# Two-layer decoder trunk: norm steps pinned to fixed places among the products, and an output projection whose second half starts with the weights still held

## The chip, the cores and the metric

The kernel runs on one core of a Trainium2 chip. The metric is the device time of one execution in microseconds (us), lower is better; the time before is the median of three runs. The core's engines are named as the profile names them: PE (TensorE, the matrix products), DVE (VectorE), ACT (ScalarE), POOL (GpSimd) and SP (SyncE, which here only issues transfers, in its own order). Each engine works through its own list of instructions in order.

## The reference, cut to what matters

```python
for l in range(2):                              # x: (1, 1024, 1024) float32
    hn = rms_norm(h, norm_mix_pre[l])
    ...                                         # l == 0: RG-LRU recurrence, l == 1: sliding-window attention -> y (768 wide)
    m_out = memory_attention(mq, mk, mv)        # 256 wide
    mixed = jnp.concatenate([y, m_out], axis=-1) @ w_out[l]
    h = h + rms_norm(mixed, norm_mix_post[l])
    f = swiglu_ffn(rms_norm(h, norm_ffn_pre[l]), w_ffn_in[l], w_ffn_out[l])
    h = h + rms_norm(f, norm_ffn_post[l])
```

Between the output projection (`w_out`) and the feed-forward stand two norms in a row: one of `mixed`, and, after the residual is added, one of `h`. Both need a sum of squares over all 1024 channels before the first feed-forward product can start on a token.

## The kernel before

**Layout.** Activations are held transposed: channels on the 128 partitions (8 tiles, index k or m), tokens along the free axis in two halves of 512 (n = 0 and 1). Every float32 product is made of three products of split operands: an operand is cast to a rounded high part (ACT, names ending in h: `ah`, `wh`, `th`, `ch`) and the rest is a subtraction (DVE, names ending in l: `al`, `wl`, `tl`, `cl`). This split is line L87 (cast) and L88 (subtraction), whatever is split. One output tile of a projection is 8 x 3 = 24 products (L147 to L149).

**Output projection (`mix_out`, `mix_half`).** For half 0 of the tokens the eight output tiles m = 0 to 7 are made in order, then for half 1 again m = 0 to 7. In layer 0 the weights of half 0 are loaded raw, split, and their parts written to memory (`keep`, tensor `kept_wo`); in half 1 all eight are fetched back (`fetch`, L190). In layer 1 all sixteen are fetched (`parted_wo`). The tiles `wh`, `wl` have two buffers in layer 0 and three in layer 1, so a fetch waits until the product block two (three) before it is done. SP issues the fetches, the residual loads (L102), the spills of the new residual (`hx`, L533) and the first feed-forward weights (`wq`, `wp`, L553) in one list.

**A norm (`rstd`)** takes five steps on four engines: DVE and ACT sum the squares; PE sums over partitions with a column of ones (`rcol`, L232, output `oo`); DVE scales (L236); POOL raises to the power -1/2 (L237); PE spreads the result over the partitions (`spread`, L244, `oo<-ident,rc...`) and ACT copies it out (L248). For each half of the tokens there are two norms: `rcp` (of `mixed`) and `rcn` (of the new residual). DVE then multiplies (`post`, L530, L532) and scales (`scaled`, L540) the eight tiles, which are split again into the operands `ah`, `al` of the feed-forward.

**Feed-forward (`ffn`).** The first products (L578 to L580) take half 0; then come two blocks of a second kind (`gated`, L599 to L601), then L578 to L580 with half 1. The two norms of half 1 have to run beside the products of half 0. `place` adds order-only dependencies by which a listed product comes behind a norm step; it doesn't hold the norm step back behind earlier products.

**Last attention units of layer 1.** Sixteen attention units (a head group for half 1 of the tokens: scores `ss` L1034, transposes `tt` L1057, output products `oo` L1064) are left when `mix_out(1)` starts. They are dealt out evenly over the eight output tiles of half 0, and `attend` runs a unit's output products when a later unit has begun.

Of the kernel before, what the change touches and what calls it, by code (L numbers as in the profile page):

```python
# [7 lines left out]
F32 = mybir.dt.float32  # L8
F32R = mybir.dt.float32r
AF = mybir.ActivationFunctionType  # L10
ALU = mybir.AluOpType
# [19 lines left out]
A_PLACES, F_PLACES, END_PLACES = (36, 54), (14, 30, 104, 116), (30, 48)  # L31
# [12 lines left out]
class Trunk:  # L44
# [12 lines left out]
    def phase(self, name, psum, *pools):  # L57
# [3 lines left out]
        self.pend, self.chain, self.where = [], None, {}  # L61
# [43 lines left out]
    def attend(self, unit=None):  # L105
        depth = self.where["qs"][1] - 1
        if unit is not None:
            self.pend.append(unit())
        while len(self.pend) > (depth if unit is not None else 0):
            self.pend.pop(0)()  # L110
# [254 lines left out]
    def mem_unit(self, q, e, kv, y):  # L365
# [21 lines left out]
        def out():  # L387
# [7 lines left out]
            for m in range(2):  # L395
                ph, pl = pts[m]
                nc.tensor.matmul(o, vv[:, m, e], pl, start=m == 0, stop=False)
                nc.tensor.matmul(o, vv[:, m, e], ph, start=False, stop=m == 1)
            self.head_out(o, y, 64 * e)

# [71 lines left out]
    def mix_split(self, y, n, order):  # L472
        act = [None] * KT
# [5 lines left out]
    def mix_half(self, layer, act, n, order, ms, f, s):  # L479
        for m in ms:  # L480
            if layer or n:
                w = self.fetch(("wo", m))
            else:
                w = self.weight(self.a["wo"][layer, m])
                self.keep(("wo", m), w)
            ps = self.proj(w, [act, act], n, ks=order)
            ft = self.acc_tile()
            self.nc.scalar.copy(ft, ps)
            if m < KT - 1:
                self.sumsq(s[0], ft, m == 0)  # L490
            else:
                s.append(self.t("sq"))
                self.nc.scalar.activation(s[1], ft, AF.Square)
            f.append(ft)

    def mix_out(self, layer, y, order, src, early=(), ld=[(f"k{h}{i}",) for h in "hl" for i in range(4)]):
        f, s, act = ([], []), [None, None], [None, None]
        hx = self.dp.tile([D, T], F32, name=f"hx{layer}")
# [7 lines left out]
        a0 = self.mix_split(y, 0, order)  # L506
        s[0] = [self.t("s")]
        us = list(early)
        for m in range(KT):
            for _ in range(-(-len(us) // (KT - m))):  # L510
                self.attend(us.pop(0))
            self.mix_half(layer, a0, 0, order, [m], f[0], s[0])
        self.attend()
        a1 = self.mix_split(y, 1, order)
        s[1] = [self.t("s")]
        self.mix_half(layer, a1, 1, order, range(2), f[1], s[1])
        finish(0, self.rstd(s[0], "p")[1], ld, "s", "rsn")
        self.mix_half(layer, a1, 1, order, range(2, KT), f[1], s[1])
# [18 lines left out]
    def scaled(self, f, rs, gain):  # L537
        act = []
# [703 lines left out]
```

## Time and profile before

| | |
|---|---|
| median of three runs (lowest, highest) | 2057.79 us (2057.29, 2061.75) |
| profiled execution | 2059.32 us |
| its span in the trace | 2057.5 us |
| mean granted PE clock over the span | 0.985 |
| instructions in the span | 27844 |

The span is the traced part of the profiled execution; about 1.8 us lie around it. A granted clock of 1 is 2.4 GHz, 0.5 is 1.2 GHz; values between are means over a stretch. Layer 0's output projection and the start of its feed-forward lie at about 255 to 400 us, layer 1's last attention units, output projection and start of the feed-forward at about 1200 to 1430 us.

### The profile page before, as it was taken

The numbers are of one execution on the slowest core, as the hardware profiler recorded it, in microseconds if no ns is written. First come the engines' busy times: TensorE is split into PE (matmuls) and PEld (weight loads), VectorE is DVE, ScalarE is ACT, GpSimd is POOL, SyncE is SP. The second block draws the span as 40 slices with busy tenths as digits, with TensorE's granted clock in tenths as the row PEclk, the third lists the DMA queues.
The fourth block names the chain that finished last, engine by engine and source line by source line (L and its number), as shares of the span: only waits on it lengthen the run. The fifth ranks groups of instructions, "written<-read, shape, count | busy, mean of one in ns | idle before, by whom it ended". The sixth has DMA issues, their size and how long they took to land.

```text
span 2057.5 us, 27844 instructions
## 1 busy us (share of the span) xinstructions
PE 1976.0 (96%) x9368; PEld 1639.0 (80%) x9368; DVE 1411.4 (69%) x2313; ACT 1022.5 (50%) x1953; POOL 483.7 (24%) x476
## 2 busy tenths in 40 slices
PE   7899999999999999999999999879999999999997
PEld 6787877788888887888788878767888888888887
DVE  7877856887677676456878776669755665664566
ACT  6757774444444444454545676644333333344551
POOL 4323420114434321000035432210122322300001
PEclk9999999999999999999999999989999999999998
DMA  5422458247677789665455314162454454686653
GB/s 170 152 84 73 140 203 307 77 159 252 233 262 246 254 284 362 212 209 169 163 195 174 134 50 165 36 236 93 149 174 136 160 172 136 204 287 194 214 182 122
DMA packets 185567, 371.68 MB, mean 181 GB/s; under 512 B 20432, under 2 KB 25808, under 8 KB 185424
## 3 DMA queue, kind: packets, MB, share of 16 engines
q1 hardware_dynamic: 185424, 369.91, 53.5%
q8 instruction: 73, 1.20, 0.2%
q14 instruction: 70, 0.57, 0.1%
HBM read 259.73 MB, written 110.10 MB: 180 GB/s over the span
## 4 chain that ended last, share of the span: by engine, by line
PE 79%; DVE 8%; ACT 4%; DMA 3%; issue 3%; POOL 2%; SPq 0%; POOLq 0%; DVEq 0%; ACTq 0%
PE mm L599 12%; PE mm L601 12%; PE mm L600 12%; PE mm L707 6%; PE mm L708 6%; PE mm L709 6%; PE mm L149 5%; PE mm L147 4%; PE mm L148 4%; PE mm L578 1%; PE mm L579 1%; PE mm L580 1%; PE oo L1064 1%; DVE acc L540 1%; DVE al L88 1%
## 5 line engine op out<-in xcount | busy, mean ns | idle before, releaser
L87 ACT CAST ch<-wq 128x512 fp32r<-128x512 f32 x311 | 193.3, 621 | 437.9 <-PE mm L600 229.2
L88 DVE TENSOR_TENSOR cl<-wq,ch 128x512 fp32r<-128x512 f32 x311 | 234.2, 754 | 193.6 <-ACT ch L87 118.8
L147 PE MATMUL mm<-al,wh 128*128 128x512 f32 x616 | 249.0, 404 | 12.4 <-DVE al L936 7.6
L149 PE MATMUL mm<-ah,wl 128*128 128x512 f32 x616 | 248.0, 403 | 5.3 <-DVE wl L88 4.0
L599 PE MATMUL mm<-al,ch 128*128 128x512 f32 x640 | 252.1, 394 | 0.0
L601 PE MATMUL mm<-ah,cl 128*128 128x512 f32 x640 | 250.8, 392 | 0.0
L600 PE MATMUL mm<-ah,ch 128*128 128x512 f32 x640 | 250.1, 391 | 0.0
L148 PE MATMUL mm<-ah,wh 128*128 128x512 f32 x616 | 246.3, 400 | 0.0
L707 PE MATMUL mm<-tl,ch 128*128 128x512 f32 x532 | 207.7, 390 | 4.0 <-DVE tl L88 4.0
L708 PE MATMUL mm<-th,ch 128*128 128x512 f32 x532 | 207.1, 389 | 0.0
L709 PE MATMUL mm<-th,cl 128*128 128x512 f32 x532 | 205.2, 389 | 0.0
L599 PE MATMUL mm<-tl,ch 128*128 128x512 f32 x480 | 188.5, 393 | 0.0
L601 PE MATMUL mm<-th,cl 128*128 128x512 f32 x480 | 188.5, 393 | 0.0
L600 PE MATMUL mm<-th,ch 128*128 128x512 f32 x480 | 187.3, 390 | 0.0
L610 DVE TENSOR_TENSOR c<-c,mm 128x512 f32<-128x512 f32 x120 | 82.4, 686 | 114.3 <-PE mm L601 114.2
L147 PEld LDWEIGHTS mm<-al,wh 128*128 128x128 f32 x616 | 118.0, 192 | 39.9 <-DVE al L936 9.7
L149 PEld LDWEIGHTS mm<-ah,wl 128*128 128x128 f32 x616 | 117.7, 191 | 33.3 <-DVE wl L88 6.6
L601 PEld LDWEIGHTS mm<-ah,cl 128*128 128x128 f32 x640 | 120.1, 188 | 28.0
L600 PEld LDWEIGHTS mm<-ah,ch 128*128 128x128 f32 x640 | 120.2, 188 | 26.5
L599 PEld LDWEIGHTS mm<-al,ch 128*128 128x128 f32 x640 | 120.2, 188 | 26.0
L148 PEld LDWEIGHTS mm<-ah,wh 128*128 128x128 f32 x616 | 118.1, 192 | 23.5
L619 POOL TENSOR_TENSOR x<-wq,wq 128x512 f32<-128x512 f32 x36 | 49.1, 1364 | 338.6 <-DMA wq<-in_wi_dram 246.9
(338 smaller groups left out, 4296.2 us busy)
## 6 DMA issues: line engine op xcount, KB each, us to landing
wq<-in_wi_dram SPq DMA_DIRECT2D x168, 256.0 KB, 4.6
xz<-hd SPq DMA_DIRECT2D x154, 256.0 KB, 4.5
th<-xz SPq DMA_DIRECT2D x154, 256.0 KB, 3.6
wp<-in_wf_dram SPq DMA_DIRECT2D x112, 256.0 KB, 4.4
wz<-wp SPq DMA_DIRECT2D x88, 256.0 KB, 2.6
wq<-wz SPq DMA_DIRECT2D x56, 256.0 KB, 3.7
wraw<-in_wa_dram SPq DMA_DIRECT2D x27, 512.0 KB, 3.5
wq<-in_wf_dram SPq DMA_DIRECT2D x42, 256.0 KB, 3.7
```

Of the source, the lines that this page charges most:

```text
L87: self.nc.scalar.copy(hi, src)
L88: return (eng or self.nc.vector).tensor_tensor(lo, src, hi.bitcast(F32), op=ALU.subtract)
L147: self.mms += [nc.tensor.matmul(out, wh, al, start=i == 0, stop=False), nc.tensor.matmul(out, wh, ah, start=False, stop=False), nc.tensor. ...
L148: nc.tensor.matmul(out, wh, ah, start=False, stop=False),
L149: nc.tensor.matmul(out, wl, ah, start=False, stop=i == len(ks) - 1)]
L599: ins += [mm(out, wh, xl, start=start and k == 0, stop=False, skip_group_check=not start), mm(out, wh, xh, start=False, stop=False, skip_g ...
L600: mm(out, wh, xh, start=False, stop=False, skip_group_check=not start),
L601: mm(out, wl, xh, start=False, stop=k == 3, skip_group_check=not start)]
L610: add = lambda o, x, y: nc.vector.tensor_tensor(o, x, y, op=ALU.add)
L707: ins += [mm(ps[m], wh[:, m], xl[:, cs], start=start and p == 0, stop=False, skip_group_check=not start), mm(ps[m], wh[:, m], xh[:, cs], s ...
L708: mm(ps[m], wh[:, m], xh[:, cs], start=False, stop=False, skip_group_check=not start),
L709: mm(ps[m], wl[:, m], xh[:, cs], start=False, stop=p == NFB // 2 - 1, skip_group_check=not start)]
```

## The change

Four edits. `F_PLACES` now pins the norm steps of the feed-forward: `pin` makes a norm step wait behind its place among the products, as well as holding the products after it. The norms of half 0 are pinned in the same way among the products of half 1 (`MIX_PLACES`). Half 1 of the output projection begins with the output tiles whose weights are still in the buffers (m = 6, 7 in layer 0, 5, 6, 7 in layer 1) and fetches only the others. The last attention units go to the first six output tiles of half 0, and their output products are placed evenly among all products of that half. `scaled` orders each scaling behind the low split two tiles before, and the residual loads of layer 0 get ten buffers in place of four. Lines of the changed kernel are numbered a little higher (L88 becomes L89, L236 becomes L237, L232 becomes L233, L244 becomes L245, L530 becomes L551, L578 becomes L601, L599 becomes L622).

```diff
-A_PLACES, F_PLACES, END_PLACES = (36, 54), (14, 30, 104, 116), (30, 48)
+A_PLACES, F_PLACES, END_PLACES = (36, 54), (10, 20, 100, 110), (30, 48)
+MIX_TAIL, MIX_PLACES = 2, (10, 20, 108, 118)
...
-            self.pend.pop(0)()
+            self.outs.append(self.pend.pop(0)())
...
+    def mix_half(self, layer, act, order, steps, f, s):
+        for i, (m, w) in steps:
+            ps = self.proj(w(m), [act], 0, ks=order)
+            f[m] = self.acc_tile()
+            self.nc.scalar.copy(f[m], ps)
...
         us = list(early)
+        self.outs, self.mms = [], []
         for m in range(KT):
-            for _ in range(-(-len(us) // (KT - m))):
+            for _ in range(-(-len(us) // max(KT - MIX_TAIL - m, 1))):
                 self.attend(us.pop(0))
-            self.mix_half(layer, a0, 0, order, [m], f[0], s[0])
-        self.attend()
-        a1 = self.mix_split(y, 1, order)
+            if m == KT - MIX_TAIL:
+                self.attend()
+            done = [order[m]] if not early else order if m == KT - MIX_TAIL else []
+            self.mix_split(y, 1, done, a1)
+            self.mix_half(layer, a0, order, [(m, (m, new))], f[0], s[0])
+        for i, g in enumerate(self.outs):
+            self.place(self.mms, [[g]], [(i + 1) * len(self.mms) // (len(self.outs) + 1)])
         s[1] = [self.t("s")]
-        self.mix_half(layer, a1, 1, order, range(2), f[1], s[1])
+        steps = [(m, lambda m: held[m]) for m in range(KT - room, KT)]
+        steps += [(m, lambda m: self.fetch(("wo", m))) for m in range(KT - room)]
+        steps = list(enumerate(steps))
+        self.mms = []
+        self.mix_half(layer, a1, order, steps[:room], f[1], s[1])
+        self.marks = []
         finish(0, self.rstd(s[0], "p")[1], ld, "s", "rsn")
-        self.mix_half(layer, a1, 1, order, range(2, KT), f[1], s[1])
+        marks = self.marks
+        self.mix_half(layer, a1, order, steps[room:], f[1], s[1])
+        for i, g in zip(MIX_PLACES, marks):
+            self.pin(self.mms, i, g)
...
     def scaled(self, f, rs, gain):
-        act = []
+        act, low = [], []
         for k in range(KT):
-            self.nc.vector.scalar_tensor_tensor(f[k], f[k], self.col(gain + k), rs, op0=ALU.mult, op1=ALU.mult)
+            ins = self.nc.vector.scalar_tensor_tensor(f[k], f[k], self.col(gain + k), rs, op0=ALU.mult, op1=ALU.mult)
+            if k > 1:
+                self.after(ins, low[k - 2])
             act.append(self.act_tile())
-            self.split(*act[k], f[k])
+            low.append(self.split(*act[k], f[k]))
...
+    def pin(self, mms, i, g):
+        self.after(g[0], mms[i - 1])
+        self.place(mms, [g], [i])
...
-        self.place(mms[0] + between + mms[1], marks, F_PLACES)
+        for i, g in zip(F_PLACES, marks):
+            self.pin(mms[0] + between + mms[1], i, g)
```

**PE, start of layer 1's feed-forward.** In these rows `mm` are feed-forward products, `oo<-ones` the two partition sums of the norm `rcp` of half 1, and `oo<-ident,rcp` its spread. Before:

```order
L244 MATMUL oo_13145<-ident,rcn_2865_13141 128x128 x4
L232 MATMUL oo_13394<-ones,s_12994 128x1 x4
L232 MATMUL oo_13394<-ones,sq_13392 128x1 x4
L244 MATMUL oo_13407<-ident,rcp_13403 128x128 x4
L578 MATMUL mm_13494<-al_13153,th_2918_13446 128x512
L579 MATMUL mm_13494<-ah_13152,th_2918_13446 128x512
```

The same place after the change, from the last product ahead of the sums to the spread:

```order
L601 MATMUL mm_13471<-al_13161,th_2920_13432 128x512
L233 MATMUL oo_13368<-ones,s_12980 128x1 x4
L622 MATMUL mm_13699<-al_13161,ch_13695 128x512
L623 MATMUL mm_13699<-ah_13160,ch_13695 128x512
L624 MATMUL mm_13699<-ah_13160,cl_13696 128x512
L233 MATMUL oo_13368<-ones,sq_13366 128x1 x4
L602 MATMUL mm_13471<-ah_13160,th_2920_13432 128x512
L603 MATMUL mm_13471<-ah_13160,tl_2921_13433 128x512
L601 MATMUL mm_13468<-al_13166,th_2908_13420 128x512
```

Before, no feed-forward product stood ahead of the sums, or between the sums and the spread. Now ten products stand ahead of the first sum, three between the two sums, and ten between the second sum and the spread. The spread of `rcn` for half 0, which stood just ahead, has moved to the middle of the output projection's half 1. Layer 0 has the same order (there, before, the spread stood behind some thirty products).

**DVE, the same norm in layer 1.** `rcp` is the short step between PE's sums and POOL's power; `acc<-acc,rsp` needs the spread result. Before:

```order
L88 TENSOR_TENSOR al_13153<-acc_11945,ah_13152 128x512
L236 TENSOR_SCALAR rcp_13403<-oo_13394 128x4
L88 TENSOR_TENSOR al_13158<-acc_12109,ah_13157 128x512
L88 TENSOR_TENSOR al_13163<-acc_12281,ah_13162 128x512
L88 TENSOR_TENSOR al_13168<-acc_12453,ah_13167 128x512
L88 TENSOR_TENSOR al_13173<-acc_12556,ah_13172 128x512
L88 TENSOR_TENSOR al_13178<-acc_12659,ah_13177 128x512
L88 TENSOR_TENSOR al_13183<-acc_12762,ah_13182 128x512
L88 TENSOR_TENSOR al_13188<-acc_12865,ah_13187 128x512
L88 TENSOR_TENSOR tl_2919_13447<-wq_13462,th_2918_13446 128x512
L88 TENSOR_TENSOR tl_2921_13449<-wq_13464,th_2920_13448 128x512
L88 TENSOR_TENSOR tl_2923_13451<-wq_13470,th_2922_13450 128x512
```

After:

```order
L89 TENSOR_TENSOR al_13196<-acc_12976,ah_13195 128x512
L89 TENSOR_TENSOR cl_13696<-wq_13687,ch_13695 128x512
L89 TENSOR_TENSOR cl_13715<-wq_13689,ch_13714 128x512
L89 TENSOR_TENSOR cl_13742<-wp_13733,ch_13741 128x512
L89 TENSOR_TENSOR cl_13761<-wp_13735,ch_13760 128x512
L237 TENSOR_SCALAR rcp_13377<-oo_13368 128x4
L551 TENSOR_TENSOR acc_13228<-acc_13228,rsp_13380 128x512
L551 TENSOR_TENSOR acc_13262<-acc_13262,rsp_13380 128x512
```

Ten subtractions that could run at once stood between `rcp` and the next step of the norm; now they stand ahead of `rcp`, and what follows it waits for the spread.

**SP, the fetches of layer 0's half 1.** `wh<-kept_wo` and `wl<-kept_wo` are the two transfers of one output tile's weights. Before, around the seventh and eighth tile:

```order
L190 DMA wh_3219<-kept_wo_2783 128x1024
L190 DMA wl_3220<-kept_wo_2783 128x1024
L533 DMA hx_2511<-acc_2811 128x512
L533 DMA hx_2511<-acc_2850 128x512
L553 DMA wq_3355<-in_wi_dram 128x512
L553 DMA wq_3357<-in_wi_dram 128x512
L190 DMA wh_3253<-kept_wo_2822 128x1024
L190 DMA wl_3254<-kept_wo_2822 128x1024
```

After, ahead of the fetch for the seventh tile of the half (m = 4):

```order
L103 DMA th_712_3483<-in_xT_dram 128x512
L103 DMA th_713_3489<-in_xT_dram 128x512
L103 DMA th_714_3496<-in_xT_dram 128x512
L103 DMA th_715_3503<-in_xT_dram 128x512
L576 DMA wq_3365<-in_wi_dram 128x512
L103 DMA tl_716_3510<-in_xT_dram 128x512
L576 DMA wq_3367<-in_wi_dram 128x512
L191 DMA wh_3205<-kept_wo_2725 128x1024
L191 DMA wl_3206<-kept_wo_2725 128x1024
```

Before, two spills and two weight loads stood between the last two fetches. Now the fetch for m = 4 stands behind residual loads and behind `wq` loads that wait for a buffer of the feed-forward.

## Rows read from the trace of the kernel before

**Rows 1.** Page, part 1: busy us, share of the span, instructions.

```profile
PE 1976.0 (96%) x9368; PEld 1639.0 (80%) x9368; DVE 1411.4 (69%) x2313; ACT 1022.5 (50%) x1953; POOL 483.7 (24%) x476
```

**Rows 2.** Waits of PE, 1335 to 1430 us: total us, times, longest.

```profile
PE oo L244 <- POOL rcp L237: 11.0, 1, 11.0
PE mm L578 <- DVE al L88: 2.7, 1, 2.7
PE oo L232 <- ACT rsn L248: 0.9, 1, 0.9
```

**Rows 3.** Timeline of PE, 1366 to 1390 us: start, duration, [idle before, releaser].

```profile
1382.11 2.08 PE L244 MATMUL oo<-ident,rcp 128*128 128x128 f32 x8 [11.04 <-POOL rcp L237]
...
1385.68 0.39 PE L580 MATMUL mm<-ah,tl 128*128 128x512 f32 x1
1385.91 0.39 PE L578 MATMUL mm<-al,th 128*128 128x512 f32 x1
```

**Rows 4.** Timeline of POOL around its two slow powers.

```profile
1375.25 6.80 POOL L237 TENSOR_TENSOR rcp<-rcp,mhalf 128x4 f32<-128x4 f32 x1 [12.04 <-DVE rcp L236]
361.95 3.80 POOL L237 TENSOR_TENSOR rcp<-rcp,mhalf 128x4 f32<-128x4 f32 x1 [19.62 <-DVE rcp L236]
```

**Rows 5.** Line L237, powers of `rcp`: ns, min/median/max.

```profile
L237 POOL TENSOR_TENSOR rcp<-rcp,mhalf x7: 1008/1020/6805, 309.8 to 1987.9; 128x4 f32<-128x4 f32 x7
```

**Rows 6.** Timeline of DVE, 1368 to 1386 us.

```profile
1369.11 5.39 DVE L540 SCALAR_TENSOR_TENSOR acc<-acc,cst,rsn 128x512 f32<-128x512 f32 x8 [6.16 <-DMA wp<-in_wi_dram]
...
1375.09 4.30 DVE L88 TENSOR_TENSOR al<-acc,ah 128x512 fp32r<-128x512 f32 x7
1379.30 1.89 DVE L88 TENSOR_TENSOR tl<-wq,th 128x512 fp32r<-128x512 f32 x3
```

**Rows 7.** Timeline of PE behind its two waits on `al`.

```profile
398.24 0.50 PE L578 MATMUL mm<-al,th 128*128 128x512 f32 x1 [2.69 <-DVE al L88]
...
1422.80 0.50 PE L578 MATMUL mm<-al,th 128*128 128x512 f32 x1 [2.69 <-DVE al L88]
...
1426.48 0.46 PE L578 MATMUL mm<-al,th 128*128 128x512 f32 x1
```

**Rows 8.** Waits of PE, 285 to 405 us (layer 0).

```profile
PE oo L232 <- ACT sq L493: 2.0, 1, 2.0
...
PE oo L244 <- POOL rcp L237: 1.5, 1, 1.5
PE oo L232 <- DVE x L222: 0.9, 1, 0.9
...
PE mm L147 <- DMA wh<-kept_wo: 0.6, 1, 0.6
PE mm L149 <- DMA wl<-kept_wo: 0.5, 1, 0.5
```

**Rows 9.** Transfers issued from 296 to 352 us: count, KB, median us to landing.

```profile
wh<-kept_wo SPq DMA_DIRECT2D x8, 512.0 KB, 4.2
wl<-kept_wo SPq DMA_DIRECT2D x8, 512.0 KB, 5.4
```

**Rows 10.** Waits of PE, 1200 to 1340 us (last attention units).

```profile
PE ss L1034 <- DVE nm L1036: 2.8, 6, 0.9
PE tt L1057 <- POOL pb L1046: 2.7, 2, 2.5
PE tt L1057 <- DVE pl L88: 2.4, 2, 2.3
PE oo L232 <- DVE acc L356: 1.4, 1, 1.4
```

**Rows 11.** Windows: us; PE, PEld, DVE, ACT, POOL busy (instructions); PE clock; DMA.

```profile
1240.00:1322.00 82.00, 76.85 (x469) 66.81 (x467) 56.88 (x178) 59.39 (x166) 21.13 (x45) 0.98 0.26 91
1322.00:1340.00 18.00, 15.49 (x76) 13.09 (x77) 8.05 (x14) 8.33 (x15) 2.65 (x5) 0.81 0.27 101
```

**Rows 12.** DVE groups, 1240 to 1322 us: output of a unit.

```profile
L356 DVE TENSOR_TENSOR acc<-oo,acc 64x512 f32<-64x512 f32 x11 | 7.5, 678 | 0.9 <-ACT acc L355 0.8
```

More of the change, by code (lines that the diff above doesn't have):

```diff
@@ L60, in phase @@
         self.stack = ExitStack()
-        self.pend, self.chain, self.where = [], None, {}
+        self.pend, self.outs, self.chain, self.where = [], [], None, {}
         pool = lambda nme, **kw: self.stack.enter_context(
@@ L397, in out @@
                 nc.tensor.matmul(o, vv[:, m, e], pl, start=m == 0, stop=False)
-                nc.tensor.matmul(o, vv[:, m, e], ph, start=False, stop=m == 1)
+                last = nc.tensor.matmul(o, vv[:, m, e], ph, start=False, stop=m == 1)
             self.head_out(o, y, 64 * e)
+            return last
         return out
@@ L470, in lru_blocks, with mix_split @@
             nc.gpsimd.tensor_tensor(gg, a2, gg, op=ALU.mult)
-    def mix_split(self, y, n, order):
-        act = [None] * KT
+    def mix_split(self, y, n, order, act=None):
+        act = [None] * KT if act is None else act
         for k in order:
@@ L477, in mix_split, with mix_out, new @@
         return act
-    def mix_half(self, layer, act, n, order, ms, f, s):
-        for m in ms:
-            if layer or n:
+    def mix_half(self, layer, act, order, steps, f, s):
[3 more added lines that the diff above has]
+            self.nc.scalar.copy(f[m], ps)
+            if i < KT - 1:
+                self.sumsq(s[0], f[m], i == 0)
+            else:
+                s.append(self.t("sq"))
+                self.nc.scalar.activation(s[1], f[m], AF.Square)
+    def mix_out(self, layer, y, order, src, early, ld):
+        f, s, act = ([None] * KT, [None] * KT), [None, None], [None, None]
+        hx = self.dp.tile([D, T], F32, name=f"hx{layer}")
+        held, room = [], self.where["wh"][1]
+        def new(m):
+            if layer:
                 w = self.fetch(("wo", m))
@@ L484, in mix_half @@
                 w = self.weight(self.a["wo"][layer, m])
[L485 to L498, printed above, removed]
+                if m < KT - room:
+                    self.keep(("wo", m), w)
+            held.append(w)
+            return w
         def finish(n, rs, ld, s, rsn):
@@ L902, in run @@
         quad = lambda i: {f"t{h}{i}{k}": 1 for h in "hl" for k in range(4)}
-        ffn = ({"mm": 7, "oo": 1}, dict(ch=4, cl=4), dict(c1=2, c6=1, c7=1, hd=7),
-               dict(x=1, wq=6, wp=4), quad(2), quad(3), quad(1))
+        ffn = ({"mm": 7, "oo": 1}, dict(ch=4, cl=4), dict(c1=2, c6=1, c7=1, hd=7, x=1),
+               dict(wq=6, wp=4), quad(2), quad(3), quad(1))
         self.phase("a", {"mm": 3, "gt": 2, "ss": 1, "tt": 1, "oo": 1}, mix_w, common, dict(rest=1),
                    dict(xr=4, graw=1, gwh=2, gwl=2, xc=2, xh=1, xl=1, gr=2, gi=2, a2=2), att)
-        mix = self.mix_out(0, *self.layer_a(), a["xT"], ld=[("xr", (P, 3 + H))])
+        spare = [("xr", (P, 3 + H)), ("gr",), ("gi",), ("a2",)]
+        mix = self.mix_out(0, *self.layer_a(), a["xT"], (), spare)
         self.phase("f0", *ffn)
@@ L1063, in out @@
             for c, (v, x, sl) in enumerate(mms):
-                nc.tensor.matmul(o[:, sl], v, x[:, sl], start=c == 0, stop=c == len(mms) - 1)
+                last = nc.tensor.matmul(o[:, sl], v, x[:, sl], start=c == 0, stop=c == len(mms) - 1)
             self.head_out(o, q, 64 * (h % 2))
+            return last
         return out
@@ L1172, in layer_b @@
         order = [6, 7, 0, 1, 2, 3, 4, 5]
-        return self.mix_out(1, y, order, self.h1, ready)
+        return self.mix_out(1, y, order, self.h1, ready, [(f"k{h}{i}",) for h in "hl" for i in range(4)])
 _INS = ["xT", "memT", "cst", "wmk", "wmv", "wa", "wg", "wo", "wi", "wf", "wk", "wv", "wb", "mask", "cos", "sin"]
```

1 line of the change is left out of this document (added).

## Prediction

> **What bounds the kernel now.** First the page's busy line: PE works 96% of the span, the next engine 69% [rows 1]. 2057.5 less 1976.0 leaves 81 us in which PE stands still, and the mean clock of 0.985 leaves about 0.015 x 1976 = 30 us lost to products at half rate. No change of order can win more than these 111 us, and only those of them that lie where the order changes. So I asked for PE's waits by stretch. The long ones crowd into three places that the change touches: the step from attention to feed-forward in layer 1 [rows 2], the same step in layer 0 [rows 8], and the last attention units [rows 10]. The reader should see one item above all: a single wait of 11.04 us on the power of `rcp`.
>
> The timelines tell why it is so long. PE had issued its partition sums and its next instruction was the spread [rows 3]. POOL's power, 1.02 us in the median of seven, took 6.80 us here, and 3.80 us in the twin of layer 0 [rows 4, 5]. While it ran, DVE did subtractions back to back from 1375.09 to 1381.19, and the power ended at 1382.05, 0.86 us after the last [rows 4, 6]. Ahead of that DVE was busy from 1369.11 with eight scalings and a subtraction [rows 6], so `rcp` itself had to queue. Each such stop has a tail. A product has a pitch of 0.23 us (1385.68 to 1385.91) [rows 3]; after the wait at 1420 us nine products took 1426.48 - 1422.80 = 3.68 us, where 9 x 0.23 = 2.07 would do [rows 7]: a loss of 1.6 us at the lower of the clock's two levels (1.2 GHz in place of 2.4).
>
> **The change part by part.**
>
> *Layer 1, attention to feed-forward.* Ten products, 2.3 us, now stand ahead of the first sum, three more ahead of the second, ten between sum and spread. The wait on `rsn`'s copy (0.9) goes: that norm moves into half 1 of the output projection. The 11.0 goes in two ways: the scalings and splits of half 0 run during half 1, some 36 products (8 us) earlier, so DVE is free for `rcp`; and behind `rcp` now stands an instruction that needs the spread, so DVE is idle while the power runs. A power at 1.02 us plus `rcp`, plus hand-overs that I put at about 0.5 us, then fits about into the 2.3 us of the ten products. The wait of 2.7 for the first `al` of half 1 goes because the split no longer queues behind eight scalings (5.39 us for eight [rows 6]) but behind two or three operations. Together 0.9 + 11.0 + 2.7 = 14.6 us [rows 2]. The slow products go with them: from 1382.11 to 1385.68, eight spreads and four products took 3.57 us, at the full rate half of it, so 1.8; and 1.6 after the other stop [rows 3, 7]. Sum **-18.0**.
>
> *Layer 0, the same step.* Waits 2.7 + 2.0 + 1.5 + 0.9 = 7.1 us [rows 7, 8], and one slow stretch behind the 2.7, taken at 1.6 like its twin: -8.7. The 0.9 for `x` is the least sure: between spread and that sum stand 80 products, 18.4 us; so the slack is a few tenths. Against it stands SP's list. The fetch for m = 4 is queued behind four `th` loads and two `wq` loads that need feed-forward buffers to come free. By following the order with the durations above I get it issued about 3.6 us before its block, and the landing takes 4.2 us for `wh` and 5.4 for `wl` [rows 9]; m = 5 is similar. I take +2, one landing's lack with little behind it; it may be nothing, or both with their slow products (below). Net **-6.7**. Four writes and four reads of 512 KB less cost nothing and are counted at nothing, since only 0.6 + 0.5 us of PE's time waits for such reads now [rows 8]. The new residual buffers only let loads start earlier, under products.
>
> *Last attention units.* Sixteen units over six output tiles in place of eight put 6 x 24 / 16 = 9 products, 2.1 us, beside each, and the last two tiles of half 0 and the first of half 1 remain as filler for the last units' chain. The end of that chain cost 2.4 (`pl`) + 1.4 (`acc`) [rows 10], and from 1322 to 1340 us the clock was 0.81 over 15.49 busy us, a loss of 2.9 [rows 11]. These go: **-6.7**. The other waits (2.8 on scores, 2.7 on `pb` [rows 10]) may shrink or grow; between -5.5 and +5 I leave them at 0, since the unit's own chain isn't changed.
>
> *Nothing for the rest:* the alternating order in `scaled` adds no instruction; it would cost a wait of one split (0.6 us, 4.30 / 7 [rows 6]) if products followed at once, which the 36 products of lead cover in half 0.
>
> Sum: -18.0 - 6.7 - 6.7 = -31.4. The profiled execution took 2059.3, so 2027.9; it lies 1.5 above the median, so 2026.4. I say **2027**. Without new waits and with the scores' and `pb`'s waits gone it is 2026.4 - 2 - 5.5 - some 4 for their clock, about 2015.
>
> **The rivals.**
>
> *Fetches.* If both late fetches cost 5.4 - 3.6 = 1.8 us each, and each stop has 1.6 us of slow products behind it, the +2 becomes +7: 2032. For it: SP's list is in strict order. Against: loads ahead of it can be ready sooner than I worked out.
>
> *Attention bound by DVE.* From 1240 to 1322 us eleven units ended [rows 12] and DVE was busy 56.88 us, 5.2 us for each; PE's 76.85 us less the share of 153 products (35 us) is 3.8 for each, and with 9 products 5.9 [rows 11]. DVE has 0.7 us in hand for each unit, less the splits of half 1 that now fall there. If chains with pinned outputs make each unit 0.8 us longer than PE's work, 16 x 0.8 = 13 us come back: 2040.
>
> *The norm stays slow, now at pinned places: slower than before.* A spread pinned ten products behind its sum stops all of PE if the power takes 6.80 again: 5.8 us beyond 1.02 and 1.6 of slow products, 7.4 each [rows 4, 5, 7]. Eight norms are pinned, 59 us if all are hit. From five hit on (37 us) the gain of 31 is gone: 2064 at six hit if nothing else changes. For it: at `rcn` of layer 0's half 0 four splits of weights follow the DVE step, 2.4 us. Against: at the other norms what follows waits for the spread or hangs on its forerunner, and the powers of such norms took 1.02 us now [rows 5]. The Trainium skill ("SBUF — State Buffer", section "Who interferes with whom") says that a VectorE instruction with two SBUF inputs and a GpSimd instruction that reads SBUF contend, and that whoever issues first holds the shared port for one whole instruction. The subtractions have two such inputs; by that rule a power would lose one subtraction at most and take about 1.7 us, which would leave this rival no price, but the row has 6.80, so the measured sum stands.
>
> *The stop only moves.* If sums or powers come later than I think, PE waits at the pins and gives back what it gains at the 11 us: 2050 to 2060. Against it: 11 us is the queue on DVE, and that is emptied in the order.
>
> **How the numbers follow.** The forecast (2014 to 2033) has 0.58, fetches at 2032 to 2036 0.12, DVE-bound units at 2034 to 2046 0.14, the moved stop 0.08, the slow power 0.08. The range takes the first three: 2014 to 2046, 0.84. What a measurement of this kernel can tell from no change is about 0.2%, 4 us. Faster: 0.84 and half of the moved stop, 0.88; same 0.04; slower 0.08.
>
> **What the profile after would show.** Right: no wait of PE on `rcp` above 1 us in either layer, all powers of `rcp` in layers' half 1 at about 1.0 us, no wait on `al` behind the gated blocks, clock near 1 from 1370 on. Waits on `wh<-kept_wo` of 1 to 2 us would show the fetch term. Wrong: powers of several us at pinned spreads; waits of the scores or outputs above 1 us for each of the last units; a new wait on `s`, `sq` or `x` at a pin.

## The result, and the profile after

| | before | after |
|---|---|---|
| median of six runs (lowest to highest) | 2059.07 us (2057.29 to 2061.75) | 2045.85 us (2040.62 to 2051.37) |
| ratio, 95% interval | 1 | 0.9933 [0.9914, 0.9952] |
| profiled execution, its span | 2059.32, 2057.5 us | 2045.31, 2043.5 us |

Medians here and below leave out two executions that took far longer than the others of their kernel (2459 us, one of a2; 4027 us, one of d2).

The change makes the kernel 13 us faster; 31 were forecast. The time lies inside the range (2014 to 2046), but at its very end, and 18 of the 31 us are missing: the prediction was wrong in size. To see where the rest went, the span is cut in three at instructions that both kernels have: the last gate product of layer 0 (`gt<-xl,gwh`), layer 1's first `vv` product, and the last product of the plain feed-forward (L578, after L601), read from first and last start of each line.

| us | layer 0, to layer 1's first `vv` | layer 1, to the last plain feed-forward product | before and behind |
|---|---|---|---|
| before | 767.7 | 407.9 | 881.9 |
| after | 768.9 | 394.6 | 880.0 |
| forecast for the step | -6.7 | -24.7 | 0 |

So layer 0 gained nothing (+1.2), and layer 1 gained 13.3 of 24.7. First the item that the forecast rested on, line L238 (L237 before) and PE's waits from 1320 to 1430 us after, to be held against [rows 2, 5]:

```profile
L238 POOL TENSOR_TENSOR rcp<-rcp,mhalf x7: 1006/1017/1028, 306.1 to 1975.7; 128x4 f32<-128x4 f32 x7
```

```profile
PE oo L233 <- ACT sq L490: 0.6, 1, 0.6
PE oo L233 <- DVE x L223: 0.5, 1, 0.5
```

No power of `rcp` takes above 1.03 us any more, and of 14.6 us of waits 0.5 at `x` is left (the 0.6 belongs to the norm of half 0, 50 us earlier). Now windows over layer 1 (columns as in [rows 11]): before, then after.

```profile
1130.00:1250.00 120.00, 114.34 (x675) 99.22 (x674) 92.82 (x240) 81.83 (x228) 44.40 (x73) 0.99 0.31 106
1250.00:1340.00 90.00, 82.34 (x491) 71.40 (x490) 59.46 (x174) 61.32 (x164) 21.93 (x45) 0.94 0.26 91
1340.00:1450.00 110.00, 95.18 (x428) 78.39 (x427) 89.79 (x146) 49.50 (x88) 9.24 (x3) 0.92 0.41 144
```

```profile
1130.00:1250.00 120.00, 110.90 (x658) 96.19 (x656) 100.22 (x264) 85.37 (x239) 48.56 (x78) 0.94 0.26 89
1250.00:1340.00 90.00, 87.06 (x505) 75.10 (x504) 60.39 (x165) 57.34 (x153) 21.38 (x41) 0.96 0.22 74
1340.00:1450.00 110.00, 109.10 (x504) 89.92 (x504) 90.39 (x146) 54.83 (x97) 6.02 (x5) 1.00 0.44 160
```

Window less PE busy is PE's idle time; busy times what the clock lacks to 1 is about the loss to slow products. In the last window idle time falls from 14.8 to 0.9 and the clock is 1.00: the forecast step. In the middle one, the end of the attention units, idle falls from 7.7 to 2.9. But in the first, where the units begin to share PE with half 0 of the projection, idle rises from 5.7 to 9.1 and the clock falls from 0.99 to 0.94 (a loss of 1.1 becomes 6.7): 9 us given back. Of these the idle time is the steady part: in eight executions below with this order (a3, a4, a6, b2, b3, c1, d1, e1) it is 8.6 to 10.8 us, while the clock there lies between 0.93 and 0.99. The clock of a window counts its idle time too, and the 11 us wait lies in the last window of before: read in windows of 5 us, its slow products are 3.3 us and not 7.6. Read so, the three windows together give 16 us less, where the stretch is 13.3 us shorter; the difference of 3 us isn't found. PE's waits from 1180 to 1330 us after name no single culprit, only the units' own chain, which nothing covers:

```profile
PE ss L1063 <- DVE nm L1065: 2.5, 5, 1.2
PE oo L1093 <- DVE pl L89: 2.5, 3, 1.8
PE tt L393 <- POOL pb L386: 1.5, 1, 1.5
PE tt L1086 <- POOL pb L1075: 0.7, 1, 0.7
```

In layer 0, windows of before, then of after:

```profile
290.00:360.00 70.00, 64.51 (x299) 52.58 (x298) 38.83 (x62) 33.11 (x59) 2.04 (x2) 0.98 0.75 270
360.00:450.00 90.00, 84.93 (x374) 69.09 (x373) 76.87 (x119) 37.48 (x65) 12.65 (x7) 0.98 0.25 86
```

```profile
290.00:360.00 70.00, 62.04 (x262) 48.49 (x261) 41.54 (x66) 32.37 (x58) 2.42 (x2) 0.93 0.61 220
360.00:450.00 90.00, 88.41 (x404) 72.28 (x403) 71.26 (x112) 38.00 (x65) 9.55 (x7) 1.00 0.23 78
```

The feed-forward's start (second window) goes from 5.1 idle and 1.7 slow to 1.6 and none: -5.2. The projection's half 1 (first window) goes from 5.5 and 1.3 to 8.0 and 4.3: +5.5. PE's waits from 285 to 405 us after, beside [rows 8]:

```profile
PE mm L148 <- DMA wh<-kept_wo: 2.3, 1, 2.3
PE mm L148 <- ACT wh L88: 1.8, 1, 1.8
PE oo L233 <- ACT sq L490: 1.3, 1, 1.3
PE mm L150 <- DMA wl<-kept_wo: 1.0, 2, 0.5
PE mm L148 <- ACT ah L88: 0.8, 1, 0.8
PE mm L148 <- ACT acc L485: 0.7, 1, 0.7
PE mm L601 <- ACT acc L485: 0.7, 1, 0.7
PE oo L233 <- DVE x L223: 0.5, 1, 0.5
```

### The profile page after: what moved, and what is told of

The parts are those of the page before. It is cut to its first block, busy times and chain, and to the rows that moved or that the text cites. A ratio compares the mean times of both kernels' runs of the same rounds, so it can differ in the third digit from the quotient of the medians.

```text
span 2043.5 us, 27804 instructions
## 1 busy us (share of the span) xinstructions
PE 1978.9 (97%) x9368; PEld 1639.0 (80%) x9368; DVE 1411.4 (69%) x2313; ACT 1021.7 (50%) x1953; POOL 479.2 (23%) x476
## 4 chain that ended last, share of the span: by engine, by line
PE 79%; DVE 9%; ACT 4%; issue 3%; DMA 3%; POOL 1%; SPq 0%; POOLq 0%; DVEq 0%; ACTq 0%
PE mm L622 12%; PE mm L624 12%; PE mm L623 12%; PE mm L730 6%; PE mm L731 6%; PE mm L732 6%; PE mm L148 5%; PE mm L149 5%; PE mm L150 5%; PE oo L1093 1%; PE tt L1086 1%; PE mm L601 1%; PE mm L602 1%; PE oo L233 1%; PE mm L603 1%
## 5 line engine op out<-in xcount | busy, mean ns | idle before, releaser
L88 ACT CAST ch<-wq 128x512 fp32r<-128x512 f32 x311 | 193.1, 621 | 423.0 <-PE mm L623 217.9
L89 DVE TENSOR_TENSOR cl<-wq,ch 128x512 fp32r<-128x512 f32 x311 | 230.7, 742 | 194.0 <-ACT ch L88 118.9
L622 PE MATMUL mm<-al,ch 128*128 128x512 f32 x640 | 252.4, 394 | 0.0
L622 PE MATMUL mm<-tl,ch 128*128 128x512 f32 x480 | 188.9, 393 | 0.9 <-DVE tl L89 0.9
L622 PEld LDWEIGHTS mm<-al,ch 128*128 128x128 f32 x640 | 120.2, 188 | 26.0
```

Source lines behind the costliest of these rows:

```text
L88: self.nc.scalar.copy(hi, src)
L89: return (eng or self.nc.vector).tensor_tensor(lo, src, hi.bitcast(F32), op=ALU.subtract)
L622: ins += [mm(out, wh, xl, start=start and k == 0, stop=False, skip_group_check=not start), mm(out, wh, xh, start=False, stop=False, skip_g ...
```

## The experiments

Each is the changed kernel with one edit, unless it says otherwise. All in one table; the stretches are those of the table above, in the run's profiled execution. The seven executions with the changed kernel's code for layer 1 (after, a3, a4, a6, c1, d1, e1) give 391.7 to 394.6 for that stretch, mean 393.4, and the four with its code for layer 0 (after, a1, a2, a5) give 767.3 to 771.0, mean 769.3: a stretch is good to about 2 us. The part before and behind, where nothing was edited, spreads from 880.0 to 883.6.

| run | median us | ratio to before, 95% | layer 0 | layer 1 |
|---|---|---|---|---|
| after | 2045.85 | 0.9933 [0.9914, 0.9952] | 768.9 | 394.6 |
| a1 outputs not placed | 2052.34 | 0.9962 [0.9950, 0.9974] | 770.0 | 398.4 |
| a2 units as before | 2052.66 | 0.9965 [0.9952, 0.9978] | 767.3 | 397.3 |
| a3 spills behind fetches | 2043.98 | 0.9922 [0.9910, 0.9934] | 769.5 | 391.7 |
| a4 sums ten later | 2041.37 | 0.9912 [0.9899, 0.9925] | 763.3 | 392.9 |
| a5 outputs after three tiles | 2043.83 | 0.9926 [0.9913, 0.9940] | 771.0 | 391.5 |
| a6 fetches on POOL's queue | 2044.12 | 0.9932 [0.9915, 0.9948] | 768.1 | 392.3 |
| b2 no pins in the feed-forward | 2055.74 | 0.9981 [0.9971, 0.9991] | 777.2 | 391.1 |
| b3 scalings in turn | 2044.86 | 0.9933 [0.9915, 0.9952] | 770.8 | 394.5 |
| c1 layer 0 as before | 2040.07 | 0.9908 [0.9895, 0.9921] | 761.6 | 394.0 |
| d1 one tile held | 2044.14 | 0.9936 [0.9924, 0.9947] | 767.5 | 394.4 |
| d2 c1 and a5 | 2035.30 | 0.9890 [0.9876, 0.9904] | 763.6 | 388.0 |
| d5 d1, a4 and a5 | 2037.89 | 0.9907 [0.9894, 0.9921] | 767.4 | 388.0 |
| e1 all fetches first | 2044.20 | 0.9937 [0.9920, 0.9954] | 768.1 | 394.0 |
| e2 e1, a4 and a5 | 2035.05 | 0.9890 [0.9877, 0.9903] | 765.7 | 388.2 |

### The attention units of layer 1: a1, a2, a5

```diff
# a1
-        for i, g in enumerate(self.outs):
-            self.place(self.mms, [[g]], [(i + 1) * len(self.mms) // (len(self.outs) + 1)])
```

> The changed kernel without the loop that places the attention units' output products among the products of half 0 in layer 1; the units still go to the first six output tiles. Theory A (the placing bars the projection's products from running ahead, so that they no longer fill the stalls of the units at 1195 to 1230 us): PE's waits between 1195 and 1230 us fall from about 7 us to about 4 and the slow products with them, and the stalls at the end of the units come back as far as filler is missing there; about 2040 to 2046 us, at the most 5 faster than the changed kernel. Theory B (the units' chain on DVE and ACT sets the pace, whatever fills PE): the waits only move, within 2 us of the changed kernel, and the sum of waits and slow products from 1195 to 1335 us stays at 15 to 18 us.

```diff
# a2: a1, and
-            for _ in range(-(-len(us) // max(KT - MIX_TAIL - m, 1))):
+            for _ in range(-(-len(us) // (KT - m))):
...
+        self.attend()
+        self.mix_split(y, 1, order if early else [], a1)
```

> The changed kernel with the last attention units dealt out over eight output tiles as before, no placing, and the splits of layer 1's half 1 behind them. Theory A (the tail edit as a whole brought nothing, it moved about 6 us of loss from the end of the units to their start): the same as the changed kernel within 3 us, with the waits at 1195 to 1230 us back at those of before (about 4) and those at the end of the units at 2.3 and 1.4. Rival (the tail edit did bring its 6.7 us and the loss lies elsewhere): 6 to 8 us slower than the changed kernel.

Both are slower than the changed kernel by 6 to 7 us in the median, but only by 3 to 4 in layer 1's stretch, and a2 was profiled in its fastest execution, 6 us below its median. By the median theory A of a2 (the edit brought nothing) falls and the rival's 6 to 8 us hold. The profiles show less: a2's idle times in the first two windows are 5.4 and 10.2 us, its clocks 0.99 and 0.92, and with the slow products that is only about 1 us more than in the changed kernel. What dealing out and placing bring in all lies between 1 and 7 us; that they bring the 6.7 of the forecast is not shown. a1 misses the times of both its theories, but its windows show the mechanism of its theory A:

```profile
1130.00:1250.00 120.00, 114.79 (x696) 100.54 (x695) 95.32 (x249) 82.18 (x229) 46.66 (x75) 0.99 0.32 112
1250.00:1340.00 90.00, 80.10 (x461) 68.39 (x460) 61.00 (x177) 59.76 (x162) 24.55 (x49) 0.91 0.11 36
```

Without the placing the first window is as before (5.2 idle, clock 0.99, 696 instructions on PE where the changed kernel had 658), and the second loses 9.9 and 7.2. The placing bars products from running ahead; taken away, they run ahead and are missing at the end: in a1's trace PE starts 168 products of the units from 1297.1 to 1333.4 us without one of the projection among them. (The windows' sums differ by 1 us from the changed kernel's. Of the 7.9 us between the two profiled executions 1.1 lie in layer 0, 3.8 in layer 1's stretch and 3.0 before and behind, where the runs spread by as much.) If the placing costs at the front and pays at the end, it should begin later:

```diff
# a5
-            self.place(self.mms, [[g]], [(i + 1) * len(self.mms) // (len(self.outs) + 1)])
+            self.place(self.mms, [[g]], [72 + (i + 1) * (len(self.mms) - 72) // (len(self.outs) + 1)])
```

> The changed kernel with the output products of layer 1's last units placed from product 72 of half 0 on (behind its first three tiles) in place of from product 10 on. Theory A (the placing from product 10 on keeps the first tiles' products from filling the stalls of the units before them, 12.6 us of waits and 5.7 of slow products from 1130 to 1250 us where there were 5.9 and 1.7): those fall to about 6 and 2, the end of the units keeps its short waits (3 + 3), and the kernel is 6 to 10 us faster than the changed one, about 2036 to 2040 us. Theory B (there are too few products for both places, so that what fills the front lacks at the end): the waits at the end rise by as much, as in the run without placing, within 3 us of the changed kernel.

```profile
1130.00:1250.00 120.00, 114.39 (x699) 100.36 (x698) 96.96 (x250) 83.50 (x234) 46.38 (x74) 0.99 0.31 106
1250.00:1340.00 90.00, 82.82 (x494) 71.10 (x494) 65.67 (x189) 61.23 (x166) 23.52 (x49) 0.96 0.18 59
```

The front is whole again (5.6 idle, 0.99). At the end 7.2 idle come back, though with few slow products (0.96). Alone the run is 1 to 2 us faster than the changed kernel, far from 6 to 10: theory B has its part. In the three other kernels with this edit the stretch is 388.0 to 388.2, so that over four executions it brings 393.4 - 388.9 = 4.5 us.

### Layer 0's output projection: c1, a4, a3, a6, d1, e1

```diff
# c1
-        held, room = [], self.where["wh"][1]
+        held, room = [], self.where["wh"][1] if layer else 0
...
-        for i, g in zip(MIX_PLACES, marks):
+        for i, g in zip(MIX_PLACES if layer else (), marks):
```

(with `steps[:room or 2]`, and one spare buffer handed to `mix_out` as before; the splits of half 1's operands stay dealt out over the tiles of half 0, as in the changed kernel)

> The changed kernel with layer 0's output projection as before (half 1 from m = 0, all eight tiles fetched, norm steps not pinned, four residual buffers); layer 1, the feed-forward pins and the order in the scalings stay. Theory A (in layer 0 the earlier norm is given back in late fetches and in the sum right behind its block, so that the edit there is worth nothing): within 2.5 us of the changed kernel. Rival (the edit in layer 0 does bring part of the 8.7 us): 4 us or more slower.

The stretch is 761.6, 7.3 us shorter than with the edit and 6.1 shorter than before, and the kernel is 5 us faster than the changed one. Neither theory said that: the edit in layer 0 isn't worth nothing, it costs some 7 us, and what stays of the change there (the pins of the feed-forward, the order of the scalings, the earlier splits) is worth 6; d2, with the same layer 0, has 763.6, so 4 to 6. PE's waits from 300 to 405 us in c1:

```profile
PE oo L233 <- DVE x L223: 1.3, 1, 1.3
PE oo L245 <- POOL rcp L238: 1.1, 1, 1.1
PE mm L601 <- ACT acc L485: 0.7, 1, 0.7
PE mm L150 <- DMA wl<-kept_wo: 0.5, 1, 0.5
PE mm L148 <- DMA wh<-kept_wo: 0.4, 1, 0.4
```

What costs? First the sum:

```diff
# a4
-        for i, g in zip(MIX_PLACES, marks):
+        for i, g in zip(MIX_PLACES if layer else (20, 30, 108, 118), marks):
```

> The changed kernel with the first norm of layer 0's half 0 pinned ten products later (20 and 30 in place of 10 and 20). Theory A (ten products of half 1 already run ahead of the last block of half 0, so the sum of sq stands right behind that block with nothing to cover the copy and the square): the wait of 1.3 us on sq at 303 us goes and 1.7 us of slow products with it, 2 to 3 us faster, unless the later norm pushes the spills and the fetch for m = 2 back by the 2.3 us of the ten products, which would give as much back. Rival (ACT is late for another reason): the wait stays.

The stretch is 5.6 us shorter, more than expected (the median 4, with intervals that overlap), and among PE's waits from 300 to 405 us the one on `sq` is gone, while the fetches still cost 4.7:

```profile
PE mm L148 <- DMA wh<-kept_wo: 3.1, 2, 2.1
PE mm L150 <- DMA wl<-kept_wo: 1.6, 3, 0.8
```

In the order of the changed kernel ten products of half 1 stand ahead of most of half 0's last block, because that block waits for its weights; the place "behind ten products of half 1" was used up before the sum's input existed, and nothing lay between block and sum. But the later norm moves the spills as well: four of them now stand behind the fetch for m = 2, which goes out at 319.95 in place of 324.11, and its wait of 2.3 us falls to 0.8. So a4 doesn't tell the sum's share of the 5.6 us from that fetch's.

Then the fetches. In the changed kernel the one for m = 2 stands behind eight spills (SP's timeline):

```profile
317.78 6.24 SPq L554 DMA_DIRECT2D hx<-acc  x8
324.11 0.54 SPq L191 DMA_DIRECT2D wh<-kept_wo  x1
```

```diff
# a3 (n = 0 of layer 0)
+        for i, d in enumerate(self.spills if not layer else []):
+            self.after(d, self.fetched[5 + 2 * (i // 4)])
```

> The changed kernel with the spills of the new residual (layer 0, half 0) ordered behind the fetches for m = 2 and m = 3 on SP. Theory A (the fetch for m = 2 was late because eight spills of 6.2 us stood ahead of it): the wait on wh<-kept_wo of 2.3 us at 328 us goes, and with it 3.1 us of slow products: 4 to 6 us faster than the changed kernel. Rival (the transfers themselves are too slow, 16 engines being busy): the wait stays above 1.5 us, within 2 us of the changed kernel.

```profile
PE mm L149 <- DMA wh<-kept_wo: 4.9, 2, 4.7
PE oo L234 <- ACT sq L491: 1.3, 1, 1.3
```

The wait for m = 2 is gone, and the fetch for m = 4 is 4.7 us late in its place: issued at 341.14, it stood behind six `wq`, four `wp` loads and three spills. The kernel is about 2 us faster, within the intervals, where theory A had 4 to 6. m = 4 is the fetch that the prediction named; in the changed kernel the wait at m = 2 had given it time.

```diff
# a6
-        steps += [(m, lambda m: self.fetch(("wo", m))) for m in range(KT - room)]
+        steps += [(m, lambda m: self.fetch(("wo", m), eng=None if layer else self.nc.gpsimd)) for m in range(KT - room)]
# d1
-        held, room = [], self.where["wh"][1]
+        held, room = [], self.where["wh"][1] if layer else 1
# e1: a3, and every load of the feed-forward in layer 0 behind a fetch
+        self.behind = [] if layer else [self.fetched[7]] * 6 + [self.fetched[9]] * 12 + [self.fetched[11]] * 8
```

> The changed kernel with layer 0's six fetches issued from POOL's queue in place of SP's, so that neither spills nor feed-forward loads stand ahead of them. Theory A (SP's order makes the fetches late): waits on kept_wo from 300 to 360 us fall below 1.5 us in sum (3.3 in the changed kernel) and the slow products behind them go: 3 to 6 us faster than the changed kernel. Theory B (the transfers are late because the 16 engines are full from 318 us on, 390 GB/s): the waits stay at 3 us or more, at other fetches, within 2 us.

> The changed kernel, but layer 0's half 1 starts with one held tile (m = 7) in place of two, and fetches seven; the early pinned norm stays. Theory A (with two buffers both held, no fetch can start until half 1's first block is done, the DMA engines stand idle from 288 to 311 us and all six fetches meet the feed-forward's loads): the first fetch is issued at about 296 to 300 us, waits on kept_wo fall below 1.5 us in sum, and layer 0 from the last gate product to layer 1's first is 4 to 7 us shorter (768.9 us in the changed kernel, 761.6 with the old projection). Rival (the early norm itself, its spills and DVE work in half 1, is what costs): that stretch stays within 2 us of 768.9.

> The changed kernel with layer 0's spills and all feed-forward loads ordered on SP behind the fetches for m = 2 to 5, as they fall due. Theory A (SP's order alone makes the fetches of the new half 1 late): no wait on kept_wo above 1 us, and layer 0 from the last gate product to layer 1's first at 760 to 764 us (768.9 in the changed kernel, 761.6 with the old projection); 5 to 9 us faster than the changed kernel. Theory B (there is too much to move between 315 and 360 us, since nothing was moved from 300 to 315): the fetches come in time but the loads behind them don't, and PE waits for th, tl or ch at the start of the feed-forward; that stretch stays at 766 us or more.

All three leave the stretch at 767.5 to 768.1, and theory A of each falls by its numbers. On POOL's queue, where nothing stands ahead of them, `wl` keeps PE waiting 4.7 us; in e1 `wh` does for 3.6 (PE's waits from 300 to 405 us: a6, then e1):

```profile
PE mm L150 <- DMA wl<-kept_wo: 4.7, 5, 1.5
```

```profile
PE mm L153 <- DMA wh<-kept_wo: 3.6, 2, 2.6
```

But e1 doesn't do what its name says. Its first six loads and the last four spills are ordered behind the fetch for m = 3, and so they still stand ahead of the one for m = 4. Four rows of its timelines: PE's last product of block m = 2, with which the buffer for m = 4 comes free; three spills and the fetch on SP; PE's first product of block m = 4:

```profile
335.39 0.39 PE L155 MATMUL mm<-ah,wl 128*128 128x512 f32 x1
334.69 2.89 SPq L562 DMA_DIRECT2D hx<-acc  x3
337.95 0.32 SPq L196 DMA_DIRECT2D wh<-kept_wo  x1
343.85 0.77 PE L153 MATMUL mm<-al,wh 128*128 128x512 f32 x1 [2.56 <-DMA wh<-kept_wo]
```

The fetch goes out 2.6 us after that product, behind three spills, and PE waits 2.56 us for it. The same reading of the other traces, for fetches on SP whose preceding block ran without a stop:

| run, fetch | last product two blocks before | fetch issued | late by | PE's wait for `wh` |
|---|---|---|---|---|
| c1, m = 5 | 327.49 | 327.68 | 0.2 | 0.4 |
| after, m = 2 | 322.19 | 324.11 | 1.9 | 2.3 |
| d1, m = 2 | 319.54 | 321.30 | 1.8 | 2.2 |
| e1, m = 4 | 335.39 | 337.95 | 2.6 | 2.6 |
| d1, m = 4 | 335.52 | 338.89 | 3.4 | 3.6 |
| a3, m = 4 | 336.41 | 341.14 | 4.7 | 4.7 |

PE's wait is, within half a us, as long as SP's list holds the fetch back, in every one of these runs, and so e1 doesn't clear the list of blame. Nor does a6: there the fetches for m = 2 to 5 go out within 0.5 us of that product, but on POOL's queue the landings take 6.6 (`wh`) and 8.0 us (`wl`), longer than a block of 24 products (5.5), so one wait was changed for another. d1 shows that the late first fetch isn't the cause: it went out at 293.45, and the waits at m = 2 and m = 4 stayed.

How full the DMA engines are shows in windows of 15 us; the last two columns are their share and GB/s. The changed kernel, then c1:

```profile
300.00:315.00 15.00, 13.66 (x65) 11.22 (x64) 3.84 (x8) 3.02 (x5) 1.03 (x1) 0.89 0.18 58
315.00:330.00 15.00, 13.21 (x58) 10.31 (x56) 12.96 (x21) 7.71 (x14) 0.00 (x0) 1.00 0.85 283
330.00:345.00 15.00, 14.44 (x57) 11.61 (x58) 6.27 (x12) 6.14 (x11) 1.40 (x1) 0.77 1.05 392
```

```profile
300.00:315.00 15.00, 15.00 (x75) 12.59 (x75) 0.16 (x1) 2.44 (x4) 1.03 (x1) 1.00 0.51 181
315.00:330.00 15.00, 15.00 (x71) 12.37 (x70) 10.88 (x18) 6.33 (x11) 0.00 (x0) 1.00 0.65 211
330.00:345.00 15.00, 14.07 (x64) 11.07 (x64) 8.41 (x14) 6.09 (x10) 1.01 (x1) 1.00 1.03 388
```

Little moves until 315 us in the new order, and from then on spills and feed-forward loads, both earlier than before, meet the fetches. But from 330 to 345 us the engines are as full in c1, whose fetches go out 0.2 to 0.7 us behind that product and cost 0.9 us. So full engines alone don't make PE wait; what differs is how much stands ahead of a fetch in SP's list. Full engines may make each entry of the list dear, which fits one row and is not shown by a run: from 336.34 to 339.09 SP issues four `th` loads of 256 KB in the changed kernel, one every 0.69 us, about the time that 256 KB take at 392 GB/s (0.67). The landings lengthen less: from 296 to 352 us they take 5.4 (`wh`) and 6.2 us (`wl`) after, for 4.2 and 5.4 before [rows 9]. No run puts every fetch ahead of the loads on SP, so what that would cost at the start of the feed-forward stays open.

### The feed-forward's pins and the order of the scalings: b2, b3

```diff
# b2
-A_PLACES, F_PLACES, END_PLACES = (36, 54), (10, 20, 100, 110), (30, 48)
+A_PLACES, F_PLACES, END_PLACES = (36, 54), (14, 30, 104, 116), (30, 48)
...
-        for i, g in zip(F_PLACES, marks):
-            self.pin(mms[0] + between + mms[1], i, g)
+        self.place(mms[0] + between + mms[1], marks, F_PLACES)
```

> The changed kernel with the feed-forward's norm steps placed as before (places 14, 30, 104, 116, without holding them back). Theory A (the 11 us went because the scalings of half 0 moved ahead and DVE is free; the pins only cover the sums): powers stay at 1.0 us, and the waits at the two sums and the spread come back at 2 to 5 us for each layer with some slow products: 4 to 10 us slower than the changed kernel. Theory B (the pins themselves removed the 11 us): a power of 3 us or more returns, and the kernel is 10 to 20 us slower, at the time of before.

```profile
L238 POOL TENSOR_TENSOR rcp<-rcp,mhalf x7: 1008/1017/1028, 307.6 to 1981.4; 128x4 f32<-128x4 f32 x7
```

10 us slower than the changed kernel, and the powers of `rcp` stay at 1.0 (longest 1028 ns): theory A. The pins are worth 10 us, but the slow power stays away without them. What removes it, b2 doesn't tell: the earlier norm of half 0 is in it, and so is the order of the scalings. In layer 0 of c1, where that norm stands as before and pins and scalings stay, it is gone as well (1.38 us, 3.80 before [rows 4]):

```profile
360.21 1.38 POOL L238 TENSOR_TENSOR rcp<-rcp,mhalf 128x4 f32<-128x4 f32 x1 [17.76 <-DVE rcp L237]
```

So in layer 0 neither the pins nor the earlier norm is needed by itself; layer 1 has no such run. The waits that come back in b2 are 2.3 us on `x` in each layer. Layer 0 is 8.3 us longer: counted in windows of 5 us, idle time is 3.2 us more and slow products 4.6, from later fetches (5.5 us of waits, 3.3 in the changed kernel), `x`, and a longer stop at 800 us. Layer 1's stretch, with the same 2077 products as the changed kernel's, is not longer: 2.7 us more idle time from 1340 to 1450 us stand against fewer slow products earlier (clocks 0.99 and 1.00 in the first two windows) in this execution.

```diff
# b3
-            if k > 1:
-                self.after(ins, low[k - 2])
```

> The changed kernel without the order in scaled (each scaling is free to run ahead of the low splits). Theory A (the wait of 2.7 us on al behind the gated blocks went because the splits no longer queue behind eight scalings): 2 to 3 us of waits on al come back in each layer with 1.6 us of slow products, 6 to 9 us slower than the changed kernel. Rival (the earlier norm alone removed it): within 3 us, no wait on al above 0.7 us.

No change in the median, and a wait on `al` of 0.8 and 0.7 us in place of 2.7: the rival holds, but for 0.1 us. The scalings' order is worth under 1 us a layer here. That the earlier norm removed the rest is not shown: in c1 layer 0 has no wait on `al` either, without the earlier norm and with the order of the scalings.

### Together: d2, d5, e2

> Two edits that were tried alone, together: layer 0's output projection as before, and layer 1's output products placed from product 72 on. If the two stretches don't touch each other: 5.3 us (the first alone) and 1.4 us (the second alone) faster than the changed kernel, about 2038 to 2040 us. If the second brings what its waits promise (24.2 us of waits and slow products from 1130 to 1340 us fell to 16.7): about 2033 us.

> Three edits together: one held tile in layer 0, the first norm there pinned ten products later, and layer 1's output products placed from product 72 on. Theory A as for the run with one held tile: layer 0 at 760 to 763 us between the last gate product and layer 1's first, and with layer 1's 391.5 about 2034 to 2039 us. If the later pin only pushes spills and fetches back: 2 to 3 us above the run with layer 0 as before and late output products.

> The same with layer 0's first norm ten products later and layer 1's output products placed from product 72 on. If theory A holds and the edits add up: layer 0 at 757 to 761 us, layer 1 at 388 to 392, about 2030 to 2034 us, faster than the run with layer 0 as before and late output products (2035.8). Under theory B: 2037 us or more.

d2 and e2 are the fastest kernels of the study, 1.1% below before and some 9 us below the changed kernel; between them there is no difference. d2 is the simpler: the old projection in layer 0, the new one in layer 1, output products placed from product 72 on. Theory A's 757 to 761 us for e2's layer 0 was not reached (765.7), so the early norm there beat the old projection in no form that was tried. d2's 2035.3 us lies near both of its sums; d5's layer 0 took 767.4, where its theory A had 760 to 763, and d5 stands 2 to 3 us above d2.

## Why the prediction was wrong, point by point

- **Layer 1's step, -18.0: right.** Idle time from 1340 to 1450 us fell by 13.9 us and the clock there is 1.00. The outcome is as read: with DVE free and idle behind `rcp` the power takes 1.02 us, and b2 shows that this holds without pins. No run leaves out the earlier norm in layer 1, so which of the edits freed DVE there stays open.
- **The wait on `al`, 2.7 in each layer: right in size, wrong in reason.** It was put on the order of `scaled`; b3 shows that beside the other edits this brings 0.7 of it.
- **Layer 0, -8.7: too high; its +2: wrong, and that is one step that failed.** c1 and d2 leave the new half 1 out and bring 6.1 and 4.1. The new half 1 costs about 7 in place of 2. Two things were mis-sized. The sum of `sq`, pinned ten products into half 1, was put at nothing ("a new wait on `s`, `sq` or `x` at a pin" was only a sign of being wrong): those ten products ran before its input existed, and it costs 1.3 us and slow products. And the fetches: the prediction followed SP's list for m = 4 and left the eight spills out, which made m = 2 late by 1.9 us and PE wait 2.3. a4 removes the first wait and most of the second and brings 5.6 of the 7; mending one fetch alone made the next one late (a3). "Four reads less cost nothing" looked at the amount, not at what stands ahead of a fetch when its buffer comes free. The rival "fetches" named the right list and priced it at +5 more; that the whole of layer 0 came to about that sum is luck, since the sum of `sq` is in it.
- **The attention units, -6.7 and "the other waits ... I leave them at 0": the second step that failed.** The end of the units gained 4.8 idle and 1.4 slow, as forecast. The front lost 3.4 idle and 5.6 slow, against a bound of 5. The order shows it: before, products of the first three tiles stand between the units; after the change PE starts 166 products of the units from 1195.6 to 1233.8 us without one of the projection, since the first output product is placed at product 10 and holds back those behind it. a1 and a5, which free the first tiles, bring the front back (5.2 and 5.6 idle, 0.99). I had compared the end of the units and not their start.
- **The rivals.** No norm was slow at a pin: the longest power of a pinned norm is 1.43 us. "Attention bound by DVE" gave nearly the right time (2040), and it alone carried the range up to 2046: that the time fell inside is luck. It named the pinned outputs, but put the loss on DVE, not on the products that the pins hold back. The price of the slow norm has a slip: 2027 + 37 = 2064 belongs to five norms hit, and six give 2071.

## What to carry to other kernels

An order that holds work back so that it fills a later gap takes it out of an earlier one: read the rows at both ends before pricing the gap that it closes. A place counted in another stream's products covers nothing if those products may run before the step's own input is made; count from the instruction that makes the input. Moving a norm earlier moves its spills and the next stage's loads too, and a fetch that just came in time before has to be priced by what stands ahead of it in its queue's list when its buffer comes free.

## What was not expected of the hardware

A stop of the same length was followed by slow products in one kernel and not in the other (a clock of 1.00 is 2.4 GHz; a mean below it holds stretches at 1.2). In the changed kernel PE waited 1.80 us for `wh` until 294.27, and the clock from 285 to 300 us was 1.00. Before, it waited 1.80 us for `wh` until 294.64 and 0.66 us more for `wl` until 296.04, and the clock from 290 to 300 us was 0.84. c1 stops for 0.90 and 0.66 us at this place, and its clock from 295 to 300 us is 0.66; so the second stop may make the difference. But the changed kernel stops once, for 1.34 us until 304.74, and has 0.66 from 305 to 310 us. No run here settles it. The runs of one kernel spread with the clock: the changed kernel took 2040.62 us in the run with mean clock 0.990 and 2051.37 in the one with 0.983.

The power next to subtractions was not slow each time. At 337.85 us in the changed kernel it took 1.40 us while four subtractions ran on DVE from 337.69 to 340.19, where [rows 4] has 6.80 and 3.80 us. No run here tells what makes the difference.
